# A weight piece's remainder on GpSimd: one subtraction of 1024 columns, or four of 256

## The chip, the cores and the metric

The kernel runs on one core of a Trainium2 chip. The metric is the device time of one execution in microseconds; a change is judged by the median of several runs. A core has TensorE (matrix products), VectorE, ScalarE and GpSimd (elementwise work), and queues that start DMA transfers between the chip's main memory and the on-chip SBUF; most of these transfers are started on SP's queue. Each engine works through its own instructions in order and waits on semaphores for the others.

## The reference: what is computed

Two layers of a diffusion backbone over 512 latent and 256 context tokens of 1024 features, in float32. In each layer:

```
h  = modulate(rms_norm(x, g_norm_attn[l]), sh1, sc1)
lat = prep_stream(h @ w_in[l], ...)          # q, k, v of three attentions, three gates
y  = (sigmoid(ga) * (y_mla @ w_up_mla) + sigmoid(gb) * (y_swa @ w_up_swa)
      + sigmoid(gc) * (y_diff @ w_up_diff)) @ w_o
x  = x + g1 * y
x  = x + g2 * (square(relu(modulate(rms_norm(x, g_norm_mlp[l]), sh2, sc2) @ w_mlp_in)) @ w_mlp_out)
```

The context tokens pass through the same weights in the first layer and are only read as keys and values in the second. The attentions are a latent attention of 8 heads, a windowed one of 8 heads with a sink, and a differential one of 4 heads.

## The kernel before, in words

Products run on float32r operands. Every float32 operand is split into a rounded half (hi) and a remainder (lo), and three products are summed in PSUM: hi with hi, hi with lo, lo with hi (lines 218 to 220 for weights that stand still, 481 to 483 for weights that move).

Weights come in pieces of 128 partitions by up to 1024 columns, made by `piece` (line 189): SP's queue loads the piece into one of two raw slots (tag wr), ScalarE copies it rounded into wh (line 197), and GpSimd subtracts that from the raw piece to give wl (line 199). There are four slots for wh and wl, so that up to four pieces are made ahead of TensorE. A piece is called for 266 times: 254 of 1024 columns, 8 of 832, 4 of 768. In the MLP a piece holds eight blocks of 128 columns, each the fixed operand of three products for each stretch of up to 512 tokens; in the projections by chunks (lines 481 to 483) it holds four blocks of 256 columns.

The work of a layer goes through four phases: projections with norms of heads and rotations (phase 1); attention, with the gate products filled in between its steps (phase 2); the three up-projections merged under the gates, and the output projection (phase 3); the MLP (phase 4), beside which the modulation of later parts is summed on VectorE (line 252).

What VectorE does between the products matters below. In attention: the maximum of the scores (line 908), the scaling of the probabilities by their sum (line 920), the difference of two maps (line 1066), the remainder of transposed probabilities (line 869). In the merge: the gate times the product (line 1232), the sum over branches (line 1238, on VectorE in the third branch and on GpSimd in the second), the remainder (line 1213). In the norms: three Newton steps of an rsqrt on a few columns (lines 443 to 454), each step needing the one before it, and the normed features (lines 431 and 434). In the MLP: the remainder of the squared activation (line 1307, behind GpSimd's square of line 1306) and the residual (line 1261).

The program is written in program order; a planner sets the order of instructions on each engine when the kernel is built, from priorities and a model of their times, and places the semaphore waits. That order is fixed when the kernel runs. Only the first norm's products are put on TensorE in an order written by hand. How the gate products are spread over the attention is set by the constants F1, WD and WC.

Of the kernel before, what the change touches and what calls it, by code (L numbers as in the profile page):

```python
"""Two layers of the hybrid diffusion backbone (MLA + windowed GQA + differential attention).

The residual stream is kept transposed (features on partitions, tokens on the free axis, latent
tokens first, context tokens after them).  Products run in float32r: every float32 operand is split
exactly into a rounded part and a remainder, and the three products that matter at float32
accuracy (hi*hi, lo*hi, hi*lo) are accumulated in PSUM.
"""
# [7 lines left out]
F32 = mybir.dt.float32  # L15
# [4 lines left out]
ALU = mybir.AluOpType  # L20
# [14 lines left out]
# columns of w_in  # L35
C_QLAT, C_KVLAT, C_KPE, C_SQ, C_SK, C_SV, C_DQ, C_DK, C_DV, C_G = (
    0, 256, 384, 416, 928, 1056, 1184, 1696, 2208, 2720)
# rope order of a head: [first halves of row and column | second halves of row and column]
# [3 lines left out]
# broadcast vectors of a layer  # L42
V_MQ, V_MK, V_SQ, V_SK, V_DQ, V_DK, V_SINK, V_L = 0, 96, 192, 256, 320, 384, 448, 456
NV = 456 + 256
# per-partition vectors of a layer
P_GA, P_GM, P_BM, P_GQ, P_GKV, P_GS = 0, 8, 16, 64, 66, 67
NP_ = 68
# constants
# [30 lines left out]
def _layout(inp):  # L79
    """Host side: permutations and concatenations only."""  # L80
    g = {n: np.asarray(a) for n, a in inp.items()}
    f = lambda a: np.ascontiguousarray(a, dtype=np.float32)
    o = {}
# [3 lines left out]
    # units of four feature blocks: shift and scale of the first norm by pairs of feature tiles, then kinds 2, 4 and 3  # L87
# [6 lines left out]
    w = g["w_in"]  # L94
# [42 lines left out]
class Build:  # L137
    def __init__(self, tc, ins, out):
        self.tc = tc
        self.nc = tc.nc  # L140
        self.ins = ins
        self.out = out
        self.n = 0
        self.mq = []
        self.early = False
        self.gains = {}
        self.F1, self.WD, self.WC = 0.3, 1.5, 0.4   # how the gates are spread over the attention
        self.px = 0

# [11 lines left out]
    def R(self, name, dt=F32):  # L161
        """a [128, 768] tile of the phase's pool"""
        return self.ph.tile([128, 768], dt, tag="R", bufs=self.NR, name=self.nm(name))
# [7 lines left out]
    def psx(self, name):  # L171
        """one bank for a dense product, from both tags in turn"""
        self.px += 1
        if self.px % 3 == 2:
            return self.psS(name)[:, 0:512]
        return self.psm(name) if self.px % 3 == 0 else self.psd(name)
# [12 lines left out]
    def piece(self, src, n=1024, own=0):  # L189
        """hi, lo of a piece of weights; own: the number of slots it takes of the phase's pool in place of the common  # L190
        ones."""
        nc = self.nc
        raw = self.sp.tile([128, 1024], F32, tag="wr", bufs=self.WR, name=self.nm("wr"))
        nc.sync.dma_start(raw[:, :n], src)
        pool, bufs = (self.ph, own) if own else (self.sp, self.WH)
        hi = pool.tile([128, 1024], F32R, tag="wh", bufs=bufs, name=self.nm("wh"))
        nc.scalar.activation(out=hi[:, :n], in_=raw[:, :n], func=AF.Copy)  # L197
        lo = pool.tile([128, 1024], F32R, tag="wl", bufs=bufs, name=self.nm("wl"))
        nc.gpsimd.tensor_tensor(out=lo[:, :n], in0=raw[:, :n], in1=hi[:, :n].bitcast(F32), op=ALU.subtract)  # L199
        return hi, lo  # L200

    def mm3(self, out, ah, al, bh, bl, start, stop):
        """out += (ah + al).T @ (bh + bl) but for al.T @ bl."""
        mm = self.nc.tensor.matmul
        mm(out, lhsT=ah, rhs=bh, start=start, stop=False)
        mm(out, lhsT=ah, rhs=bl, start=False, stop=False)
        mm(out, lhsT=al, rhs=bh, start=False, stop=stop)
# [5 lines left out]
    def dense_steps(self, ps, w, x, c):  # L213
        """ps = sum of w.T @ x[:, c]; w: [(hi, lo)] stationary [128, 128] blocks, x: [(hi, lo)] moving."""
# [8 lines left out]
    def split_sb(self, src, n=768):  # L223
        """hi, lo of an SBUF tile."""
# [7 lines left out]
    def mod_start(self, kinds):  # L232
        """queue up mod = silu(c) @ w_mod + b_mod for the given sixths, features on partitions."""
# [27 lines left out]
    def mod_pe(self, w, ks, ps):  # L261
        """ps[32 g + stream, 128 features] += 2 silu(c) @ w for four feature blocks g; w [128, len(ks), 512]."""
# [7 lines left out]
    def mod_out(self, ps, pt):  # L270
        """[128 features, 4 blocks, 32]: twice the modulation without its bias."""
# [5 lines left out]
    def mod_first(self, q):  # L277
        """shift and scale of the first norm for feature tiles 2q and 2q + 1, in two steps."""
# [18 lines left out]
    def mod_units(self, n):  # L297
        """n pieces of the modulation of kinds 2, 4 and 3 of the first layer."""
# [18 lines left out]
    def first_norm(self, x, h):  # L317
        """the first norm, feature tiles as their modulation arrives, and the query latent of the first layer: PSUM
        tiles [128 tokens, 256]."""
# [45 lines left out]
    def norm_gain(self, l, which, s, k=None):  # L365
        """128 * g * (1 + scale) per feature (rows_rsq gives 1 / 128); of feature tiles k and k + 1 alone at every even k."""
# [19 lines left out]
    def add_square(self, acc, x, j, c, sq, eng):  # L386
        """acc += x_j ** 2 on columns c; sq: a scratch tile."""
# [7 lines left out]
    def rows_rsq(self, sq, nt, ones, s=None):  # L395
        """sq [128 features, nt * 128 tokens] of squares -> [128, nt * 128]: rsqrt(mean + eps) of the tokens on the
        diagonal of every block, with eps * s ** 2 if the rows are s times too large. ones: column constant 1 / number
        of features."""
# [11 lines left out]
    def rows_bcast(self, dg, nt, name):  # L410
        """PSUM [128, nt * 128]: the diagonals of dg / 128 on all partitions."""
# [7 lines left out]
    def norm_apply(self, acc, x, h, c, gain, shift, hold):  # L419
        """h = split(x * rsqrt(mean) * gain + shift) on columns c; hold: the last scratch tiles take the slots of the  # L420
        modulation's weights, whose stream then starts after the norm."""
# [16 lines left out]
    def rsq_small(self, ss, n, d, s=None):  # L438
        """rsqrt(ss / d + eps) on [128, n]; rsqrt(ss + eps * s ** 2) if s is given."""
# [17 lines left out]
    def sumsq(self, raw, m, d):  # L457
        """sum of squares of raw [128, m * d] over d."""
# [12 lines left out]
    def bproj(self, act, w, n, tiles, evac):  # L471
        """act: [(hi, lo)] per k with tokens on the free axis; w: [(hi, lo)] per k, [128, n]."""
# [20 lines left out]
    def rope_pairs(self, raw, npair, nt, tab, gain):  # L493
        """raw [128, npair, nt, 2, 64]: gain and rotation of the latent tiles, gain alone of the context tiles."""
# [18 lines left out]
    def phase1(self, l, h, nq, pre):  # L513
# [5 lines left out]
        # rope tables with the gains in  # L519
# [22 lines left out]
        # MLA tables: [C | S] for q and k, 32 wide  # L542
# [26 lines left out]
        # q latent  # L569
# [11 lines left out]
        # kv latent, shared rope key, SWA keys and values  # L581
# [14 lines left out]
        def lora(raw, kts, nt, gcol):  # L596
            """raw [128 tok, nt, kts * 128] -> normalised, transposed and split."""
# [22 lines left out]
        # SWA keys  # L620
# [5 lines left out]
        # shared rope key  # L626
# [15 lines left out]
        def chunk256(ci, tiles):  # L642
            """a chunk of 256 columns of w_in, as [128, 2 pairs, tiles, 128]."""
# [25 lines left out]
        # MLA keys and values  # L669
        kw = []  # L670

        def ukv(ci):
# [16 lines left out]
            # ss index (pair, t, h)  # L689
# [20 lines left out]
        # MLA queries  # L710
# [48 lines left out]
        # P: what the attention needs for its first head  # L759
# [13 lines left out]
    def transp(self, tok, w, nt, evac):  # L773
        """token tiles of tok [128, nt, w] transposed; evac(ps, cols) for every PSUM bank."""
# [27 lines left out]
    def q_pair(self, tok, nt):  # L802
        """stacks [hi; lo] of head 0 and [lo; hi] of head 1."""
# [10 lines left out]
    def k_pair(self, d):  # L814
        """[hi; hi] and [lo; lo] of both heads of d: every head is loaded twice."""
# [19 lines left out]
    def v_heads(self, tok):  # L835
        """[hi | lo] of the two heads of a pair [128, 6, 128]."""
# [15 lines left out]
    def p_transpose(self, p, kts, PT, q2):  # L852
        """blocks kts of p (at column order of kts) into PT hi/lo [128, 6, 256] at half q2."""
# [19 lines left out]
    def pv2(self, v, PT, kts, y, rows, c):  # L873
        """y[rows, c] = (v_hi + v_lo).T @ (p_hi + p_lo) with v = [hi | lo]."""
# [28 lines left out]
    def exp_rows(self, ps, c0, sums):  # L903
        """exp(s - max) and its sums."""
# [23 lines left out]
    def mla_job(self, sc, hd, nq, st):  # L928
        """closures of a head: prep, units [(front, back)], ends."""
# [37 lines left out]
    def swa_job(self, l, sc, hd, nq, st):  # L967
# [16 lines left out]
        def unit(b):  # L984
# [17 lines left out]
            def front():  # L1002
                # the products are -s: p holds mask - s with -sink in front of it, the minimum is minus the maximum of the scores
# [30 lines left out]
    def diff_job(self, l, sc, hd, nq):  # L1034
# [16 lines left out]
        def unit(i):  # L1051
# [5 lines left out]
            def front():  # L1057
                # -s1 (p1 / s1 - lam p2 / s2): the norm of the head takes s1 out again, gsub the sign
# [46 lines left out]
    def gate_steps(self, l, h, nq, gates):  # L1105
        """tanh(logit / 2) of all gate features, kept in DRAM; yields after every step of three products."""
# [21 lines left out]
    def phase2(self, l, h, sc, nq, job, st):  # L1128
# [13 lines left out]
        def fill(t):  # L1142
            """dense work of t us between the steps of the attention"""
# [62 lines left out]
    def merge(self, l, br, ys, yh, gates, m, nq, psum):  # L1206
        """m += (1 + tanh) * (y @ w_up) for a branch; the last one returns 0.5 * m split, the others the next y split."""
# [55 lines left out]
    def out_proj(self, l, mh, x, nq, done):  # L1263
        """x += g1 * (m @ w_o); the last feature tiles run half by half; done(acc, c) after each half."""
# [28 lines left out]
    def mlp(self, l, h, x, nq, pre, fin, done):  # L1293
        """x += g2 * relu(h @ w_mlp_in) ** 2 @ w_mlp_out; fin(j, c) when x[j][:, c] is final."""
# [66 lines left out]
    def build(self):  # L1361
        tc, nc, ins = self.tc, self.nc, self.ins
        import contextlib
        with contextlib.ExitStack() as es:
# [13 lines left out]
            # conditioning  # L1378
            nc.scalar.preload_act_table_set("exp_and_others")
            # 2 silu(c) with the rows of w_mod on partitions  # L1380
# [96 lines left out]
    def norm(self, l, which, x, acc, h, c, hold=False):  # L1477
        """h[:, c] = modulated norm of x[:, c]"""
# [4 lines left out]
    def layer_consts(self, l):  # L1483
        """per-layer vectors, the lambda of the differential maps and the gain of their norm."""
# [45 lines left out]
```

## Time and profile before

| what | value |
| --- | --- |
| median of 3 runs | 2549.3 us (2545.8 to 2554.59) |
| span of the profiled execution | 2547.0 us |
| time of that execution around its span | not given apart; the median of the runs stands 2.3 us above the span |
| mean granted TensorE clock | 0.988 |
| instructions | 40061, of these GpSimd 629 |
| VectorE, ScalarE, GpSimd busy | 1537.6, 1079.7, 915.1 us |
| line 199 (the subtraction) | 266 instructions, 652.6 us |

In the profile PE is TensorE, PEld its weight loads, DVE VectorE, ACT ScalarE, POOL GpSimd and SPq SP's queue. An instruction's time runs from its start on the engine to its end, so time in which an engine is held up inside an instruction counts as busy. A row's releaser (after the arrow in brackets) is what ended the idle time before it. The granted clock is 1.00 at 2.4 GHz and 0.50 at 1.2 GHz.

### The profile page before, as it was taken

To read this page: it belongs to the slowest core of one execution; us is meant where nothing else is said; L and a number is where in the kernel's file an instruction comes from. 1 tells how busy PE (TensorE), PEld (TensorE's weight loads), DVE (VectorE), ACT (ScalarE), POOL (GpSimd) and SP (SyncE) were. 2 spreads that over 40 slices of the span, in tenths; PEclk is the share of its full clock that TensorE was granted. 3 is DMA by queue.
4 is the path that set the end of the run, shared out by engine and by line. 5 is a ranking of instruction groups with operands and counts; after the bars stand their busy time and mean duration, and the time that the engine had idled before them with its cause. 6 is when DMAs were issued, how large, how long until landed. Compare 5 with 4: busy or idle time off the path is not lost. (4 is left out here: it accounts for less than half of the span.)

```text
span 2547.0 us, 40061 instructions
## 1 busy us (share of the span) xinstructions
PE 2432.5 (96%) x15466; PEld 2136.6 (84%) x15466; DVE 1537.6 (60%) x3081; ACT 1079.7 (42%) x2105; POOL 915.1 (36%) x629
## 2 busy tenths in 40 slices
PE   6999999999999998999999989999999999999999
PEld 5989888888888887888888989998878777888888
DVE  6547777878874479872222277777788874621112
ACT  4343566667652233212222244346666632422321
POOL 2434211111115326434333354441222235454543
PEclk9999999999999999999999999999999999999999
DMA  7265322222346225662111122443323344222222
GB/s 280 90 222 203 131 97 84 96 77 94 100 137 226 94 76 171 214 231 75 59 67 66 60 99 86 173 153 95 103 83 118 110 156 155 83 92 99 91 100 83
DMA packets 133182, 307.38 MB, mean 121 GB/s; under 512 B 43264, under 2 KB 49536, under 8 KB 132608
## 3 DMA queue, kind: packets, MB, share of 16 engines
q1 hardware_dynamic: 122624, 281.23, 32.6%
q10 hardware_dynamic: 10368, 23.60, 2.4%
q8 instruction: 122, 2.00, 0.3%
q14 instruction: 68, 0.56, 0.1%
HBM read 252.08 MB, written 52.70 MB: 120 GB/s over the span
## 5 line engine op out<-in xcount | busy, mean ns | idle before, releaser
L199 POOL TENSOR_TENSOR wl<-wr,wh 128x1024 fp32r<-128x1024 f32 (+2 forms) x266 | 652.6, 2457 | 1139.2 <-ACT wh L197 1066.8
L197 ACT ACTIVATE wh<-wr 128x1024 fp32r<-128x1024 f32 (+2 forms) x266 | 279.5, 1052 | 581.2 <-PE mo L219 317.6
L218 PE MATMUL mo<-uh,wh 128*128 128x512 f32 (+1 forms) x832 | 286.4, 344 | 18.6 <-DVE x L1261 13.6
L219 PE MATMUL mi<-hl,wh 128*128 128x512 f32 (+1 forms) x832 | 285.7, 344 | 3.3 <-DVE hl L434 3.3
L220 PE MATMUL mi<-hh,wl 128*128 128x512 f32 (+1 forms) x832 | 285.2, 343 | 0.0
L218 PE MATMUL mi<-hh,wh 128*128 128x512 f32 (+1 forms) x832 | 284.8, 344 | 0.3 <-DVE x L1261 0.3
L219 PE MATMUL mo<-ul,wh 128*128 128x512 f32 (+1 forms) x832 | 283.8, 341 | 0.0
L220 PE MATMUL mo<-uh,wl 128*128 128x512 f32 (+1 forms) x832 | 283.1, 341 | 0.0
L1307 DVE TENSOR_TENSOR ul<-u,uh 128x512 fp32r<-128x512 f32 (+1 forms) x104 | 80.7, 777 | 304.0 <-POOL u L1306 301.7
L1261 DVE SCALAR_TENSOR_TENSOR x<-mo,mod,x 128x512 f32<-128x512 f32 (+1 forms) x208 | 127.9, 625 | 200.6 <-PE mo L220 200.6
L481 PE MATMUL pb<-wh,hh 128*128 128x256 f32 (+1 forms) x832 | 244.2, 294 | 0.0
L482 PE MATMUL pb<-wl,hh 128*128 128x256 f32 (+1 forms) x832 | 243.2, 292 | 0.8 <-POOL wl L199 0.8
L483 PE MATMUL pb<-wh,hl 128*128 128x256 f32 (+1 forms) x832 | 243.3, 293 | 0.0
L218 PE MATMUL g<-hh,wh 128*128 128x512 f32 (+1 forms) x576 | 212.2, 368 | 0.0
L220 PE MATMUL g<-hh,wl 128*128 128x512 f32 (+1 forms) x576 | 211.8, 368 | 0.0
L219 PE MATMUL g<-hl,wh 128*128 128x512 f32 (+1 forms) x576 | 211.5, 367 | 0.0
L868 ACT ACTIVATE pth<-pT 128x512 fp32r<-128x512 f32 (+3 forms) x344 | 154.1, 462 | 101.7 <-PE pT L865 90.4
L218 PEld LDWEIGHTS mo<-uh,wh 128*128 128x128 f32 x832 | 157.3, 189 | 39.1 <-DVE x L1261 14.9
L869 DVE TENSOR_TENSOR ptl<-pT,pth 128x512 fp32r<-128x512 f32 (+3 forms) x344 | 171.9, 516 | 24.8 <-ACT pth L868 22.6
L219 PEld LDWEIGHTS mi<-hl,wh 128*128 128x128 f32 x832 | 157.3, 189 | 23.5 <-DVE hl L434 3.7
L218 PEld LDWEIGHTS mi<-hh,wh 128*128 128x128 f32 x832 | 156.8, 189 | 20.4 <-DVE x L1261 0.5
L220 PEld LDWEIGHTS mi<-hh,wl 128*128 128x128 f32 x832 | 157.3, 189 | 19.8
(243 smaller groups left out, 5932.5 us busy)
## 6 DMA issues: line engine op xcount, KB each, us to landing
wr<-in_wmi SPq DMA_DIRECT2D x64, 512.0 KB, 3.5
wr<-in_wmo SPq DMA_DIRECT2D x64, 512.0 KB, 3.5
wm<-in_wmod SPq DMA_DIRECT2D x56, 512.0 KB, 3.6
wr<-in_wg SPq DMA_DIRECT2D x48, 512.0 KB, 3.6
wr<-in_wb SPq DMA_DIRECT2D x36, 512.0 KB, 4.2
wm<-in_wm SPq DMA_DIRECT2D x28, 512.0 KB, 4.5
wr<-in_wup SPq DMA_DIRECT2D x24, 512.0 KB, 3.5
gd<-gt ACTq DMA_DIRECT2D x24, 384.0 KB, 2.4
```

What stands on the lines that cost most here:

```text
L197: nc.scalar.activation(out=hi[:, :n], in_=raw[:, :n], func=AF.Copy)
L199: nc.gpsimd.tensor_tensor(out=lo[:, :n], in0=raw[:, :n], in1=hi[:, :n].bitcast(F32), op=ALU.subtract)
L218: mm(ps, lhsT=wh, rhs=xh[:, c], start=i == 0, stop=False)
L219: mm(ps, lhsT=wh, rhs=xl[:, c], start=False, stop=False)
L220: mm(ps, lhsT=wl, rhs=xh[:, c], start=False, stop=i == n - 1)
L481: mm(ps[:, :n], lhsT=ah[:, cs], rhs=wh, start=k == 0, stop=False)
L482: mm(ps[:, :n], lhsT=ah[:, cs], rhs=wl, start=False, stop=False)
L483: mm(ps[:, :n], lhsT=al[:, cs], rhs=wh, start=False, stop=k == nk - 1)
L868: nc.scalar.activation(out=hv[:, k0:k0 + n, qs], in_=pv, func=AF.Copy)
L869: nc.vector.tensor_tensor(out=lv[:, k0:k0 + n, qs], in0=pv, in1=hv[:, k0:k0 + n, qs].bitcast(F32), op=ALU.subtract)
L1261: self.nc.vector.scalar_tensor_tensor(out=x[j][:, c], in0=ps, scalar=g, in1=x[j][:, c], op0=ALU.mult, op1=ALU.add)
L1307: nc.vector.tensor_tensor(out=b[:, c], in0=u, in1=a[:, c].bitcast(F32), op=ALU.subtract)
```

## The change

The subtraction of line 199 is put into a loop over blocks of 256 columns. A piece of 1024 columns takes four instructions on GpSimd, one of 832 takes four (the last of 64 columns), one of 768 takes three. The load and ScalarE's copy stay whole. Comments and docstrings are taken out as well, which changes nothing in the program.

```
         lo = pool.tile([128, 1024], F32R, tag="wl", bufs=bufs, name=self.nm("wl"))
-        nc.gpsimd.tensor_tensor(out=lo[:, :n], in0=raw[:, :n], in1=hi[:, :n].bitcast(F32), op=ALU.subtract)
+        for o in range(0, n, 256):
+            c = slice(o, min(o + 256, n))
+            nc.gpsimd.tensor_tensor(out=lo[:, c], in0=raw[:, c], in1=hi[:, c].bitcast(F32), op=ALU.subtract)
         return hi, lo
```

## Rows read from the trace of the kernel before

**Rows 1.** The page's busy times by engine: us, share of the span, instructions.
```profile
PE 2432.5 (96%) x15466; PEld 2136.6 (84%) x15466; DVE 1537.6 (60%) x3081; ACT 1079.7 (42%) x2105; POOL 915.1 (36%) x629
```

**Rows 2.** Windows by stage: length, busy us of each engine, clock, DMA share, GB/s.
```profile
0.00:260.00 260.00, 230.92 (x2158) 217.01 (x2159) 163.07 (x373) 105.92 (x204) 98.86 (x93) 0.99 0.55 198
345.00:745.00 400.00, 389.22 (x2599) 339.97 (x2597) 321.90 (x771) 264.52 (x612) 67.57 (x61) 1.00 0.29 95
1005.00:1115.00 110.00, 94.39 (x514) 81.58 (x514) 95.78 (x137) 22.19 (x32) 45.94 (x22) 0.94 0.63 212
1470.00:1640.00 170.00, 151.44 (x1081) 147.75 (x1080) 134.36 (x296) 74.33 (x157) 82.59 (x79) 0.95 0.34 119
1640.00:2075.00 435.00, 420.13 (x2666) 356.78 (x2665) 344.36 (x708) 266.16 (x550) 118.31 (x93) 0.99 0.35 113
2075.00:2180.00 105.00, 98.44 (x472) 80.70 (x473) 51.76 (x74) 27.79 (x38) 50.33 (x27) 0.95 0.43 148
2200.00:2547.00 347.00, 343.89 (x1630) 286.42 (x1628) 79.97 (x114) 100.58 (x133) 176.68 (x94) 1.00 0.27 94
```

**Rows 3.** TensorE's waits: us in total, times, longest.
```profile
PE pm L266 <- DVE acc L393: 15.2, 1, 15.2
...
PE pb L482 <- POOL wl L199: 0.8, 2, 0.6
```

**Rows 4.** Timeline around a stall at 744: start us, us, what [idle before].
```profile
741.77 2.42 POOL L199 TENSOR_TENSOR wl<-wr,wh 128x1024 fp32r<-128x1024 f32 x1 [14.76 <-PE s L893]
...
742.18 2.29 DVE L1066 SCALAR_TENSOR_TENSOR p<-p,sm,p 128x256 f32<-128x256 f32 x1
...
745.12 0.39 PE L205 MATMUL o<-pth,vh 128*128 128x256 f32 x1 [1.31 <-DVE ptl L869]
```

**Rows 5.** Four VectorE lines: count, ns at least/median/at most, first and last start.
```profile
L1066 DVE SCALAR_TENSOR_TENSOR p<-p,sm,p x40: 484/1016/2287, 616.5 to 2060.4; 128x768 f32<-128x768 f32 x32, 128x256 f32<-128x256 f32 x8
...
L1238 DVE TENSOR_TENSOR m<-m,tl x16: 691/960/3128, 821.9 to 2134.3; 128x768 f32<-128x768 f32 x8, 128x512 f32<-128x512 f32 x8
...
L1232 DVE SCALAR_TENSOR_TENSOR tl<-tl,up x48: 406/678/689, 788.2 to 2133.5; 128x512 f32<-128x512 f32 x32, 128x256 f32<-128x256 f32 x16
...
L453 DVE SCALAR_TENSOR_TENSOR a<-a,v x135: 145/168/2340, 20.4 to 2194.9; 128x24 f32<-128x24 f32 x36, 128x6 f32<-128x6 f32 x24, 128x16 f32<-128x16 f32 x24, 128x2 f32<-128x2 f32 x24
```

**Rows 6.** GpSimd's groups by form: busy us, mean ns | idle before.
```profile
L199 POOL TENSOR_TENSOR wl<-wr,wh 128x1024 fp32r<-128x1024 f32 x254 | 628.3, 2476 | 1114.9 <-ACT wh L197 1045.6 <-DVE q L811 22.5 <-PE pT L865 17.0
...
L393 POOL TENSOR_TENSOR acc<-acc,sq 128x256 f32<-128x256 f32 x19 | 14.3, 754 | 16.9 <-ACT sq L392 10.8 <-ACT acc L390 5.7
```

**Rows 7.** Timeline of GpSimd and VectorE, 1557.7 to 1561.5, GpSimd instructions back to back.
```profile
1557.70 0.71 POOL L503 TENSOR_TENSOR rt<-raw,tab 128x256 f32<-128x256 f32 x1
1557.79 0.65 DVE L453 SCALAR_TENSOR_TENSOR a<-a,v 128x4 f32<-128x4 f32 x1
1558.38 0.71 POOL L504 TENSOR_TENSOR rt<-raw,tab 128x256 f32<-128x256 f32 x1
1558.48 0.64 DVE L454 SCALAR_TENSOR_TENSOR y<-a,y 128x4 f32<-128x4 f32 x1
...
1559.74 1.71 POOL L504 TENSOR_TENSOR rt<-raw,tab 128x256 f32<-128x256 f32 x1
```

**Rows 8.** The page's groups of two of the three products.
```profile
L219 PE MATMUL mo<-ul,wh 128*128 128x512 f32 (+1 forms) x832 | 283.8, 341 | 0.0
L220 PE MATMUL mo<-uh,wl 128*128 128x512 f32 (+1 forms) x832 | 283.1, 341 | 0.0
```

**Rows 9.** Timeline of VectorE within the stall at 1015.
```profile
1014.02 3.24 DVE L252 CUSTOM_DVE_ANT_0 dump<-wm,silu 128x1024 bf16<-128x1024 f32 x1
```

**Rows 10.** Timeline of TensorE behind the first and last of thirteen stalls.
```profile
1717.27 0.38 PE L881 MATMUL o<-pth,vv 128*128 128x256 f32 x1 [0.57 <-DVE ptl L869]
...
2065.98 0.39 PE L205 MATMUL o<-pth,vh 128*128 128x256 f32 x1 [1.47 <-DVE ptl L869]
```

**Rows 11.** Window of the low clock behind the stall at 2134.
```profile
2134.35:2141.18 6.83, 3.69 (x9) 2.63 (x9) 3.91 (x3) 2.32 (x3) 2.82 (x2) 0.50 0.23 79
```

## The prediction

> **What bounds the kernel.** Read the busy shares first: TensorE works 2432.5 of the 2547.0 us span, VectorE 60%, GpSimd 36% [rows 1]. So the order of the matmuls sets the time, and all that a change off TensorE can give back is the 114.5 us in which TensorE stands still, plus what a lowered clock costs. Next the windows by stage [rows 2], where the length minus TensorE's busy time is what to look at: 29.1 us idle in the first 260 us, 10.8 in 345 to 745 (layer 0's attention), 15.6 in 1005 to 1115 (the head of its MLP), 18.6 in 1470 to 1640 (the crossing to layer 1), 14.9 in 1640 to 2075 (layer 1's attention), 6.6 up to its output projection, 3.1 in its MLP; the stretches between hold the other 15.9. Then TensorE's own waits [rows 3]: 15.2 us are the start, before any weight piece, and for the remainder piece that the change touches TensorE waits 0.8 us in all. The weight supply is not what ends last.
>
> What does end last is VectorE. The timeline of one stall [rows 4] shows the pattern: the subtraction runs from 741.77 to 744.19; a VectorE update of 256 columns starts at 742.18 and is over at 744.47, just behind it; the next VectorE instruction feeds TensorE, which has stood for 1.31 us. The same line takes 0.48 us at its fastest, and the sum of line 1238 goes from 0.69 to 3.13 us, while line 1232, which reads PSUM as one input, never passes 0.69 [rows 5]. So a VectorE instruction that reads SBUF twice is held until the GpSimd instruction in progress has ended; the scaling of line 920, with one SBUF input, behaves alike. Going through TensorE's stalls of over 0.4 us, I find an instruction held by line 199 in front of most of them.
>
> **The change, part by part.** *Removed:* 266 subtractions, 254 of them of 1024 columns at 2.476 us. *Added:* four blocks for each piece of 1024 or 832 columns, three for 768. The nearest row of 256 columns on GpSimd is the sum of line 393, 0.754 us [rows 6]. So 4 x 0.754 = 3.02 for 2.48, 0.54 more a piece; over 254 pieces 137 us, and some 5 for the other 12: GpSimd goes from 915 to about 1057 us, 41% of the span. From the other side, back-to-back instructions of 256 columns start every 0.68 us [rows 7]: 2.72 a piece, 61 us more in all. I take the larger. It lies beside matmuls: a piece of an MLP feeds 24 products and more, of 0.21 us each in layer 1 (343.89 us over 1630 matmuls [rows 2]), 5.1 us, against 3.0 of GpSimd for the piece and about 1.1 for the piece's share of line 1306; and the first block is ready 0.75 us after the start where its columns came after 2.48. If that cover were gone, the cost would be up to 142 us; with 0.8 us of waits now I price it at nothing.
>
> *More waits on TensorE:* up to three more points a piece, some 800, at which line 220 and its like wait for GpSimd; all later matmuls queue behind such a wait. Today line 220 does so in one product of 13, line 219 never, and both last 341 ns with no idle time ahead [rows 8]: a wait that cost 13 ns would show as 1. So 0, at most 10 us; I take 0. *Queues:* the raw slot is let go 0.54 us later, and the next piece load on SP with it, with other loads behind it in that queue; the pieces in store cover that, 0 (the 142 us above if not).
>
> *What the stalls get back.* Held by a subtraction of 2.4 us, an instruction waits 1.2 us on average; held by a block of 0.75, 0.4, if VectorE comes in between two blocks. Rows 7 answer that: with GpSimd instructions of 0.71 us back to back, VectorE gets one instruction through for each (0.65 and 0.64 us, where such updates take 0.15 alone [rows 5]), and GpSimd waits in turn for a long VectorE one (1.71). So a single held instruction gains; a run of small dependent ones, as the steps of an rsqrt, does not: it is held once a block, 4 x 0.5 = 2.0 us, where it was held once for up to 2.2. Going through the stalls by that rule, estimates from the timeline:
> - 0 to 260: small chains and loads, -2 of 29.1.
> - 345 to 745: four stalls each behind one held scaling, two behind other single ones, -6.5 of 10.8; two more stand behind the unchanged subtraction of line 1046.
> - 1005 to 1115: the largest stalls (11.5 us) are a queue of modulation sums of 1.2 us, held to 3.2 [rows 9]; a dense stream alternates with blocks, so 0 there, and -2.5 of three later ones.
> - 1470 to 1640: -2.5 of 18.6, the rest being rsqrt runs, table work and results that wait for ScalarE.
> - 1640 to 2075: thirteen stalls behind a held instruction, the first of 0.57 us, the last of 1.47 [rows 10], -9.5 of 14.9.
> - 2075 to 2180: the sums of line 1238, held while the next product waits for the split of their result, -4 of 6.6.
> - Between these (two norms, a merge): -5 of 15.9.
>
> That is -32. *The clock:* behind the stall at 2134 the granted clock is 0.50, 1.2 GHz of 2.4, for 6.8 us in which nine matmuls pass [rows 11]; 1005 to 1115 stands at 0.94, 1470 to 1640 and 2075 to 2180 at 0.95 [rows 2]. Some of these stretches should go with their stalls, -5. *What comes back:* a stall removed brings the next VectorE result closer, and GpSimd holds on for 142 us more; I keep 70%: (32 + 5) x 0.7 = 26, and give one back for the rsqrt runs. The span goes from 2547.0 to 2522; the runs' median stood 2.3 us above that span: 2524.
>
> **A rule against it.** The Trainium skill, "GPSIMD Engine Reference", section Instruction dispatch, says that consecutive GpSimd instructions are no barrier: each of its cores takes up the next as soon as its own share is done. By that rule four blocks could hold the shared port like one instruction of 3 us; that is the first rival. Rows 7 speak against it here, since VectorE comes through once in each instruction of 0.71 us.
>
> **The rivals.**
> - *Held for the whole piece.* Blocks follow so closely that VectorE doesn't get in, and each hold grows from 2.48 to 3.02 us, by 22%. The stalls that follow VectorE, some 75 us (114.5 less the 15 at the start and some 25 behind loads, ScalarE and the end), grow with it: +17, 2566. It decides from the point at which no slot is left between two blocks. The one-for-one alternation of rows 7 is against it; that no four blocks of one piece are in this trace is for it. 0.11.
> - *One stall for another.* In dense stretches VectorE is hit by every block: four holds of 0.4 us are 1.6 a piece, more than one of 1.2. If streams and rsqrt runs set most stalls, what the single ones gain is spent there: 2549. For it speak 1005 to 1115 and 1470 to 1640 (34.2 us idle); against it, that some 25 stalls elsewhere have one held instruction each. 0.18.
> - *Nearly all goes.* A hold of 0.4 us falls within the lead that the filling products give, where 1.2 did not, and the clock stays up: two thirds of the 75 us, and some 5 of clock: 2495. The lengths in layer 1's attention (0.57 to 1.47 us) speak for it, the rsqrt runs against. 0.15.
> - The forecast, 2510 to 2541: 0.56.
>
> More GpSimd instructions may also put others in another order, on every engine; no row prices that, and it is in the width.
>
> **How the numbers follow.** 0.3% is 7.6 us, about what can be told from no change. Faster: the forecast and the large gain, 0.71; no difference: 0.18; slower: 0.11. The time is 2524. The range reaches down into the large gain and up over no change: 2498 to 2552.
>
> **What would show it.** Right: four times as many instructions of line 199, of about 0.75 us, and GpSimd near 1050; the longest instructions of lines 920, 1066, 1238 and 434 below 1.7 us; TensorE's idle time in 1640 to 2180 from 21.5 to below 11; lines 452 to 454 no better in sum; the clock at 1.00 in more of the stages. Wrong: VectorE instructions held for 2 us across several blocks; TensorE waiting for wl; as much idle time in new places, or matmuls in another order.

## The result, and the profile after

The changed kernel takes 2518.4 us (median of four runs, 2517.3 to 2521.0) against 2549.3 us. The ratio is 0.988 with a 95% interval of 0.986 to 0.989. The forecast was 2524. The profiled execution has a span of 2517.3 us against 2547.0. TensorE's matmuls stand in the same order in both traces. The planner moved some other instructions: on VectorE between 960 and 1160 us (layer 0's MLP) and within the norm at 1520, on SP two loads from 1140 us to 1018 and 1045, and a pair each at three places on ScalarE (742, 1525 and 2214 us of the kernel before). In the kernel after, line numbers from 200 on are higher by two (L1238 is L1240); in the kernels of the experiments they are as before.

The busy times by engine, with VectorE and GpSimd as [rows 1] have them:

```profile
PE 2425.4 (96%) x15466; PEld 2132.4 (85%) x15466; DVE 1498.0 (60%) x3081; ACT 1078.8 (43%) x2105; POOL 1102.9 (44%) x1423
```

GpSimd has 188 us more (1102.9 less 915.1) and VectorE 40 us less, for the same work: its instructions are held for shorter times. TensorE stands still for 91.9 us of the span, where it was 114.5 us, and is busy for 7.1 us less, at a higher mean granted clock (0.992 instead of 0.988). That is the 29.7 us.

The windows by stage follow. The stages are those of [rows 2], shifted so that each holds the same matmuls to within a few; columns are the length, busy us of each engine, clock, DMA share, GB/s.

```profile
0.00:262.00 262.00, 233.16 (x2159) 218.41 (x2160) 160.80 (x377) 106.03 (x204) 116.56 (x169) 0.99 0.55 196
346.00:742.00 396.00, 390.20 (x2603) 340.66 (x2601) 316.76 (x770) 264.46 (x611) 77.73 (x124) 1.00 0.29 96
1000.00:1108.00 108.00, 93.76 (x519) 80.78 (x518) 92.27 (x144) 22.29 (x32) 72.37 (x59) 0.95 0.67 226
1463.00:1625.00 162.00, 148.03 (x1079) 144.02 (x1080) 122.73 (x287) 74.25 (x157) 96.79 (x139) 0.97 0.33 114
1625.00:2056.00 431.00, 418.35 (x2667) 357.42 (x2666) 339.36 (x718) 265.22 (x550) 142.41 (x199) 0.99 0.36 118
2056.00:2152.00 96.00, 94.11 (x476) 78.58 (x476) 44.85 (x72) 28.14 (x39) 61.07 (x69) 1.00 0.47 162
2170.00:2517.00 347.00, 344.19 (x1632) 286.60 (x1631) 90.10 (x115) 100.86 (x133) 202.36 (x274) 1.00 0.27 94
```

The lengths go 260 to 262, 400 to 396, 110 to 108, 170 to 162, 435 to 431, 105 to 96, and 347 in both. So the crossing to layer 1 and the output projection before its MLP gave most, and the first stage lost. The low clock behind the stall at 2134 [rows 11] is gone: that stage runs at 1.00 instead of 0.95.

The VectorE lines of [rows 5] (count, ns at least/median/at most), and with them the norm's product L436:

```profile
L1068 DVE SCALAR_TENSOR_TENSOR p<-p,sm,p x40: 484/1012/2615, 614.5 to 2041.6; 128x768 f32<-128x768 f32 x32, 128x256 f32<-128x256 f32 x8
...
L1240 DVE TENSOR_TENSOR m<-m,tl x16: 691/960/1268, 818.7 to 2108.7; 128x768 f32<-128x768 f32 x8, 128x512 f32<-128x512 f32 x8
...
L436 DVE SCALAR_TENSOR_TENSOR hl<-nt,mod,hh x64: 464/481/970, 905.2 to 2173.3; 128x256 fp32r<-128x256 f32 x64
...
L455 DVE SCALAR_TENSOR_TENSOR a<-a,v x135: 147/174/726, 20.2 to 2165.3; 128x24 f32<-128x24 f32 x36, 128x6 f32<-128x6 f32 x24, 128x16 f32<-128x16 f32 x24, 128x2 f32<-128x2 f32 x24
```

Read the last of the three numbers. The sum of L1238 fell from 3.13 to 1.27 us at most, the rsqrt step from 2.34 to 0.73. L1068 still goes to 2.62: it stands there behind the unchanged subtraction of L1048, which lasts 1.85 us.

The stall of [rows 4], the same matmuls (start us, us, what, idle before):

```profile
739.28 3.01 POOL L201 TENSOR_TENSOR wl<-wr,wh 128x256 fp32r<-128x256 f32 x4 [14.33 <-PE s L895]
...
740.29 0.71 DVE L1068 SCALAR_TENSOR_TENSOR p<-p,sm,p 128x256 f32<-128x256 f32 x1
...
740.92 1.01 DVE L871 TENSOR_TENSOR ptl<-pT,pth 128x512 fp32r<-128x512 f32 x2
...
741.66 0.39 PE L207 MATMUL o<-pth,vh 128*128 128x256 f32 x1 [0.32 <-DVE ptl L871]
```

The four blocks take 3.01 us, and inside them VectorE gets its update done in 0.71 us where it took 2.29; TensorE waits 0.32 us instead of 1.31.

GpSimd's group of the changed line (busy us, mean ns | idle before), and a line of the products beside it that answers to [rows 8]:

```profile
L201 POOL TENSOR_TENSOR wl<-wr,wh 128x256 fp32r<-128x256 f32 x1060 | 847.2, 828 | 1014.5 <-ACT wh L197 959.4
...
L222 PE MATMUL mo<-uh,wl 128*128 128x512 f32 (+1 forms) x832 | 282.4, 340 | 0.0
```

The product pays nothing for its three more points of waiting: 340 ns as before (341). TensorE's waits (us in total, times, longest) show what is new:

```profile
PE pm L268 <- DVE acc L395: 14.9, 1, 14.9
PE mo L220 <- DVE x L1263: 12.6, 5, 10.0
...
PE tp L782 <- DMA ld<-km: 8.0, 2, 5.7
```

The 5.7 us is a stall that the kernel before did not have, at 1680: layer 1's first head waits for its keys. Timeline of GpSimd, VectorE and SP ahead of it, and of TensorE at its end:

```profile
1673.78 3.97 POOL L201 TENSOR_TENSOR wl<-wr,wh 128x256 fp32r<-128x256 f32 x5
1674.29 0.71 DVE L445 TENSOR_SCALAR v<-ss 128x16 f32<-128x16 f32 x1
1675.04 0.65 DVE L449 TENSOR_SCALAR y<-v 128x16 int32<-128x16 int32 x1
...
1677.12 0.66 DVE L455 SCALAR_TENSOR_TENSOR a<-a,v 128x16 f32<-128x16 f32 x1
1677.82 0.17 DVE L456 SCALAR_TENSOR_TENSOR y<-a,y 128x16 f32<-128x16 f32 x1
...
1679.28 1.22 DVE L470 TENSOR_TENSOR raw<-raw,y 128x1024 f32<-128x1024 f32 x1
1680.53 0.80 SPq L667 DMA_DIRECT2D qs<-raw  x2
...
1682.42 0.81 SPq L792 DMA_DIRECT2D ld<-km  x1
...
1686.46 0.84 PE L782 MATMUL tp<-identr,ld 128*96 128x128 f32 x6 [5.75 <-DMA ld<-km]
```

Two pieces, eight blocks, run there without a pause until 1677.8, and the steps of an rsqrt are held once a block: five in a row of 0.65 to 0.71 us, and 0.17 us each as soon as GpSimd stops. The product of L470 is late by that, a store of SP waits for it (the longest such wait of SP here is 5.1 us), and the loads of the head stand behind that store in SP's queue.

### The profile page after: what moved, and what is told of

Same layout as the page of the kernel before. It is cut to its first block, busy times and chain, and to the rows that moved or that the text cites. A ratio compares the mean times of both kernels' runs of the same rounds, so it can differ in the third digit from the quotient of the medians.

```text
span 2517.3 us, 40953 instructions
## 1 busy us (share of the span) xinstructions
PE 2425.4 (96%) x15466; PEld 2132.4 (85%) x15466; DVE 1498.0 (60%) x3081; ACT 1078.8 (43%) x2105; POOL 1102.9 (44%) x1423
## 5 line engine op out<-in xcount | busy, mean ns | idle before, releaser
L201 POOL TENSOR_TENSOR wl<-wr,wh 128x256 fp32r<-128x256 f32 x1060 | 847.2, 828 | 1014.5 <-ACT wh L197 959.4
L220 PE MATMUL mo<-uh,wh 128*128 128x512 f32 (+1 forms) x832 | 285.7, 343 | 15.6 <-DVE x L1263 12.6
L1309 DVE TENSOR_TENSOR ul<-u,uh 128x512 fp32r<-128x512 f32 (+1 forms) x104 | 96.1, 926 | 296.4 <-POOL u L1308 291.4
```

Of the source, the lines that this page charges most:

```text
L201: nc.gpsimd.tensor_tensor(out=lo[:, c], in0=raw[:, c], in1=hi[:, c].bitcast(F32), op=ALU.subtract)
L220: mm(ps, lhsT=wh, rhs=xh[:, c], start=i == 0, stop=False)
L1309: nc.vector.tensor_tensor(out=b[:, c], in0=u, in1=a[:, c].bitcast(F32), op=ALU.subtract)
```

## The experiments

*Theory T1, as forecast:* a VectorE instruction is held until the GpSimd instruction in progress ends, so the length of that instruction is what counts. *Rivals:* the number of instructions or the planner's new order did it (R1); the first block being ready sooner did it (R2). A second question came from the stall at 1680 and became the main one: is GpSimd's longer time free, as I had priced it (T2), or does it cost something (R3)?

**Instructions of uneven length.** Four instructions a piece again, three of 64 columns and one of 832, so that the number is as in the change and the longest hold nearly as before.

```
-  tensor_tensor(out=lo[:, :n], in0=raw[:, :n], in1=hi[:, :n], op=subtract)
+  for c in [slice(0,64), slice(64,128), slice(128,192), slice(192,n)]: tensor_tensor(out=lo[:, c], ...)
```

> Blocks of 64, 64, 64 and the remaining 832 columns: as many GpSimd instructions and semaphore points for a piece of 1024 as with four of 256, but one of them still holds VectorE for about 2 us. Every instruction of TensorE, VectorE, ScalarE and SP stands in the order of the kernel before. Theory of the hold (the time follows how long the longest GpSimd instruction keeps VectorE out): hardly any gain, 2540 to 2552. Rival, the number of instructions and the finer waits: near 2518 as with the four even blocks. If the 0.2 us of each further instruction cost something by themselves, over 2552.

Measured: 2542.6 us, ratio 0.996 (0.994 to 0.998). The sums and the norm's product in its trace:

```profile
L1238 DVE TENSOR_TENSOR m<-m,tl x16: 691/958/2682, 820.7 to 2131.2; 128x768 f32<-128x768 f32 x8, 128x512 f32<-128x512 f32 x8
...
L434 DVE SCALAR_TENSOR_TENSOR hl<-nt,mod,hh x64: 468/480/2248, 908.2 to 2200.2; 128x256 fp32r<-128x256 f32 x64
```

Single instructions of 2.2 and 2.7 us are back, where the same work takes 0.5 and 0.7 alone (2.6 and 3.1 were the longest in the kernel before), and most of the gain is gone. The number of instructions falls as a cause: as many of them, another length, 24 us apart. The planner's order is not settled by this run, for its kernel has the order of the kernel before on TensorE, VectorE, ScalarE and SP. The run with two blocks, below, bears on it.

**The blocks backwards.** As the change, the last 256 columns first; the columns that the first products want come last.

```
-  for c in [slice(o, min(o + 256, n)) for o in range(0, n, 256)]: ...
+  for c in [slice(o, min(o + 256, n)) for o in range(0, n, 256)][::-1]: ...
```

> The four blocks of 256 columns in reversed order, so that the columns that TensorE takes first are ready last. Theory of the hold: 2515 to 2523, as in the changed kernel (2518). Rival, the first block is ready early (0.75 us in place of 2.4) and that feeds TensorE: the gain goes back, 2535 to 2550, and TensorE waits for wl.

Measured: 2518.9 us, ratio 0.988 (0.985 to 0.991), the same as forwards. R2 falls.

**Two blocks of 512 and eight of 128.** The same line with another step.

```
-  ... range(0, n, 256) ...
+  ... range(0, n, 512) ...     (two)
+  ... range(0, n, 128) ...     (eight)
```

> Two blocks of 512 columns, each about 1.3 us. Theory of the hold: between the two, in proportion to the length of the hold 2549 - 31 x (2.40 - 1.29) / (2.40 - 0.74) = 2528, so 2522 to 2534; held VectorE instructions at most 1.3 us over their own time. Rival, any split does it: 2518. Rival, only a hold below some slack counts: 2540 and more.

Measured: 2526.9 us, ratio 0.991 (0.989 to 0.994), the longest of L1238 1.82 us, GpSimd 985 us: between one block and four, as the length of the hold has it. Its order is that of the change on TensorE and SP, and on VectorE but for a few instructions of the norm at 1520; yet it takes 8 us more. And in layer 0's attention and from 1640 us to layer 1's MLP, where 18 of the 30 us were gained, the change moved no more than one pair, on ScalarE. So the order is not what did it there; for the crossing and the head of layer 0's MLP, where instructions did move, the two are not told apart by stage. With that R1 falls for most of the gain.

> Eight blocks of 128 columns, each about 0.45 us (GpSimd some 1.0 us more per piece than with one). Theory of the hold alone: 2549 - 31 x (2.40 - 0.45) / (2.40 - 0.74) = 2512, so 2508 to 2517. Rival, the longer time of a piece on GpSimd and the later release of raw slots to SP's loads eats the rest: 2518 to 2530, with waits of TensorE for wl or for loads behind it.

Measured: 2527.6 us, ratio 0.991 (0.989 to 0.994), GpSimd 1298 us. The holds are shorter in sum than with four (VectorE has 44 us less; the longest rsqrt step, 0.78 us, and the longest of L434, 0.97, are as there), yet it is slower. One instruction was kept out for long:

```profile
2089.27 4.73 DVE L1238 TENSOR_TENSOR m<-m,tl 128x512 f32<-128x512 f32 x1
2090.07 3.38 POOL L199 TENSOR_TENSOR wl<-wr,wh 128x128 fp32r<-128x128 f32 x8
```

The first row's 4.73 us spans all eight blocks of a piece: VectorE did not get in between any of them. It is the only one of its 16 at that length, and it can't explain 9 us alone. (The last section has more such cases.) So shorter holds stop paying between 256 and 128 columns, and something that grows with the number of blocks takes it back: GpSimd's time is the candidate (R3).

**Four blocks again, and the first heads' loads on ScalarE's queue.** A run of the change beside three variants.

> The change as it is (four blocks of 256), beside the next three on the same chip: 2518, as before within 4 us. In its trace the loads of layer 1's first head stand behind a piece load in SP's queue and TensorE waits some 5.7 us for them at 1680.

Measured: 2520.8 us, ratio 0.988 (0.986 to 0.989).

```
-  self.nc.sync.dma_start(t[:, :n], d)
+  (self.nc.scalar if self.early else self.nc.sync).dma_start(t[:, :n], d)
```

> Four blocks, and the loads for the first head of each layer's attention started on ScalarE's queue in place of SP's, so that they don't stand behind piece loads that wait for GpSimd to release a raw slot. Theory (the later release of raw slots makes these loads late): the waits of TensorE for these loads (5.7 in layer 1, some 2 to 3 in layer 0) go, 2509 to 2514, that is 4 to 9 below the four blocks. Rival, the loads come as late for another reason (their source is written late), or ScalarE's queue takes the place: no difference to the four blocks.

Measured: 2518.6 us, ratio 0.987 (0.985 to 0.989): the intervals overlap. Its TensorE waits:

```profile
PE pb L481 <- ACT raw L650: 3.6, 1, 3.6
PE tp L780 <- DMA ld<-km: 2.9, 1, 2.9
```

The stall at layer 1's loads, 6.4 us in the run beside it, is gone (the 2.9 us is the one at layer 0's first head, 2.2 there), and a wait for a ScalarE result of 3.6 us came in its place, 50 us earlier. ScalarE's rows ahead of that wait:

```profile
1625.79 0.36 ACTq L790 DMA_DIRECT2D ld<-vm  x1
1626.61 0.39 ACT L650 ACTIVATE raw<-pb 128x256 f32<-128x256 f32 x1 [9.01 <-DVE raw L468]
```

ScalarE stands for 9.0 us and goes on right behind the load, where in the run beside it line 650 runs from 1618.9 us on. So the stall goes through SP's queue, but taking it away is not worth 6 us: the loads hold up ScalarE instead. (The planner also put 119 matmuls in another order in this kernel, some of them at 1620 to 1714.)

**The other subtraction in blocks too.** The change, and line 1046 in three blocks.

```
-  nc.gpsimd.tensor_tensor(out=vl, in0=vt, in1=vh, op=subtract)
+  for c in (slice(0,256), slice(256,512), slice(512,768)): nc.gpsimd.tensor_tensor(out=vl[:, c], ...)
```

> Four blocks, and the other long subtraction on GpSimd (the remainder of the values in the differential attention, 8 times 768 columns, 1.85 us) in three blocks of 256. The order on TensorE, VectorE, ScalarE and SP is that of the four blocks. Theory of the hold: the two stalls behind it in layer 0 (0.4 and 1.1 us) shorten, some 1 us in all, 2514 to 2519. Rival: nothing.

Measured: 2514.6 us, ratio 0.986 (0.984 to 0.988). It is the fastest median of all, as the theory wants, but its interval overlaps that of four blocks alone; the gain is not shown.

**One block twice.** The change, and the last block of each piece done once more: 0.75 us more of GpSimd a piece, with no longer hold.

```
-  for c in [... range(0, n, 256)]: ...
+  for c in [... range(0, n, 256)] + [slice(n - 256, n)]: ...
```

> Four blocks of 256 and the last one once more: the length of a hold as with four, but a piece takes 0.75 us more of GpSimd, some 200 us in all, as much as eight blocks of 128 took (1298 us of GpSimd against 1103). If eight blocks lost their 9 us by the longer time of a piece on GpSimd: 2523 to 2532 here too, and waits for wl as there (8.6 us). If they lost it by VectorE being kept out across several short blocks: 2515 to 2522 here.

Measured: 2569.2 us, ratio 1.007 (1.005 to 1.009). Both expectations were far off: 48 us above four blocks, and 42 above eight, with nearly eight's GpSimd time. The page:

```profile
PE 2448.5 (95%) x15466; PEld 2149.9 (84%) x15466; DVE 1522.9 (59%) x3081; ACT 1079.1 (42%) x2105; POOL 1323.3 (52%) x1689
```

TensorE idles 119.4 us (91.7 in the four blocks beside it) and is busy for 23 us more (2425.2 there), at a lower mean granted clock (0.982 instead of 0.992). Either GpSimd's time costs that much, and eight blocks earned it back by their shorter holds, or the block written twice at the end is special. Four more kernels tell this apart.

*The first block twice, ahead of the others.*

```
+  for c in [slice(0, min(256, n))] + [... range(0, n, 256)]: ...
```

> Four blocks of 256 columns, and the FIRST block is done once more ahead of them (five had the last one once more: 2569, the same GpSimd time as the eight blocks of 128, which took 2528). The repeated work writes what it wrote before. Theory T (it is GpSimd's time itself: some 210 us more of 256-column instructions make whatever stands behind them on GpSimd late, and eight blocks only paid it back with shorter holds): 2560 to 2575, as five. Rival L (in five the piece's end was late because the last columns were written twice, one behind the other): 2520 to 2535.

Measured: 2568.2 us, ratio 1.008 (1.006 to 1.009), as with the last one. Which block of the piece is done twice makes no difference.

*Eight blocks, the last two twice.*

```
+  for c in [... range(0, n, 128)] + [... range(max(n - 256, 0), n, 128)]: ...
```

> Eight blocks of 128 columns, and the last two of them once more: to the eight blocks what five is to four, a repeated 256 columns, in instructions of 128. GpSimd some 1540 us. T: eight (2528) plus what the repeat cost on four (some 48 us): 2565 to 2585. Rival H (what the repeat costs is one more hold of VectorE of .75 us a piece, and short instructions hold it less): 2532 to 2548.

Measured: 2579.5 us, ratio 1.012 (1.011 to 1.014), 52 us above eight: the same 256 columns cost as much in instructions of half the length. So the price is not that of one more hold of 0.75 us. Four VectorE instructions in its trace are held over six blocks and more (the last section); TensorE has no stall of over 0.3 us behind three of them and 1.5 us in all beside the fourth, so they are not the price either.

*The kernel before, the last 256 columns twice.*

```
-  tensor_tensor(out=lo[:, :n], ...)
+  for c in [slice(0, n), slice(max(n - 256, 0), n)]: tensor_tensor(out=lo[:, c], ...)
```

> The kernel before (the whole piece in one instruction), and the last 256 columns once more behind it. GpSimd some 1110 us, as with four blocks, but with holds of 2.4 us still. T: 2549 plus some 45: 2585 to 2605. Rival H: the long holds are there as before, one of .75 is added: 2552 to 2575.

Measured: 2596.3 us, ratio 1.020 (1.017 to 1.022), 48 us above the kernel before. The price was there already, before anything was cut.

*Four blocks, the last 64 columns twice.*

```
+  for c in [... range(0, n, 256)] + [slice(max(n - 64, 0), n)]: ...
```

> Four blocks of 256, and the last 64 columns once more: some .31 us a piece, 82 us of GpSimd in all, against 210 in five. T, in proportion to GpSimd's time: 2520 plus 48 x 82/210 = 2539 (2533 to 2545). If the price is only paid beyond some spare time of GpSimd at single places: 2518 to 2528. If it is paid by the number of instructions or by the rewriting as such: 2555 to 2572.

Measured: 2536.9 us, ratio 0.996 (0.995 to 0.998): it goes with GpSimd's time, not with the number of instructions.

The page's VectorE and GpSimd times of the last three:

```profile
PE 2448.4 (95%) x15466; PEld 2146.2 (83%) x15466; DVE 1495.4 (58%) x3081; ACT 1078.9 (42%) x2105; POOL 1550.8 (60%) x3007
```

```profile
PE 2444.1 (94%) x15466; PEld 2143.0 (83%) x15466; DVE 1593.0 (62%) x3081; ACT 1080.0 (42%) x2105; POOL 1143.6 (44%) x895
```

```profile
PE 2434.7 (96%) x15466; PEld 2138.7 (84%) x15466; DVE 1497.2 (59%) x3081; ACT 1080.1 (43%) x2105; POOL 1210.7 (48%) x1689
```

Against the kernel that each stands on, by spans and GpSimd's busy time: the last block twice +51.0 us for +228 (2567.9 less 2516.9; 1323.3 less 1095.1), the first block twice +49.0 for +228, eight blocks +50.9 for +253, the kernel before +42.4 for +229, the 64 columns +17.4 for +116. That is 0.15 to 0.22 us for each us. T2 falls, R3 holds.

One more thing differs in these five kernels: the planner's order. Up to 28 matmuls at the head of layer 1's MLP moved by one or two places (2160 to 2174 us), VectorE's and SP's order changed in layer 0's MLP, VectorE's also in a norm or two, and SP's in a few places behind 1620 us. The price can't be only that. Ahead of 950 us TensorE, VectorE and SP run in one order in both of each pair, and by there the kernel with one block twice is 16.7 us behind four blocks, the one with the first block twice 17.4, eight blocks with two more 16.0 behind eight, the kernel before with its block 11.7 behind the kernel before, and the 64 columns 8.2 behind four. For the rest the order may have a part in the price.

*Where it is paid.* The windows of the kernel with one block twice, from the start to layer 0's attention, at the head of its MLP, at the crossing, in layer 1's attention and up to its output projection:

```profile
0.00:354.00 354.00, 317.76 (x2713) 293.04 (x2714) 223.70 (x501) 152.64 (x309) 168.16 (x228) 0.97 0.50 175
1012.00:1129.00 117.00, 96.69 (x515) 82.98 (x515) 95.77 (x148) 22.45 (x32) 83.64 (x74) 0.91 0.66 216
1485.00:1659.00 174.00, 152.34 (x1077) 148.00 (x1078) 125.71 (x287) 74.16 (x157) 111.24 (x156) 0.94 0.31 105
1659.00:2099.00 440.00, 422.96 (x2669) 360.69 (x2669) 347.09 (x718) 265.46 (x550) 173.43 (x237) 0.98 0.36 116
2099.00:2201.00 102.00, 97.72 (x470) 80.12 (x470) 45.40 (x70) 27.50 (x38) 73.44 (x84) 0.97 0.45 152
```

and of the four blocks beside it, the same matmuls:

```profile
0.00:342.00 342.00, 312.48 (x2715) 288.80 (x2716) 219.10 (x501) 152.08 (x309) 138.06 (x196) 0.99 0.52 181
996.00:1104.00 108.00, 92.81 (x513) 80.05 (x512) 89.26 (x141) 21.50 (x31) 69.59 (x58) 0.95 0.67 223
1459.00:1623.00 164.00, 149.75 (x1080) 146.17 (x1081) 121.27 (x287) 74.27 (x157) 95.98 (x139) 0.96 0.33 113
1623.00:2054.00 431.00, 418.10 (x2665) 357.04 (x2664) 339.69 (x718) 265.49 (x550) 140.35 (x199) 0.99 0.37 118
2054.00:2151.00 97.00, 94.44 (x471) 78.51 (x472) 46.08 (x71) 27.52 (x38) 60.50 (x69) 1.00 0.47 160
```

The lengths differ by 12, 9, 10, 9 and 5 us, 45 of the 51, at a lower clock in each; the rest of the two MLPs costs next to nothing (0.0 and 0.9 us). Only a small part of it is TensorE waiting for wl itself:

```profile
PE pb L482 <- POOL wl L199: 8.3, 7, 4.0
```

That wait has 8.3 us against 2.5 in the four blocks. The largest wait that grew is on SP: its piece loads wait for the subtraction that lets a raw slot go. First the kernel with one block twice, then the four blocks, then the eight (SP's waits: us in total, times, longest):

```profile
SPq L194 <- POOL wl L199: 892.9, 227, 12.7
```

```profile
SPq L194 <- POOL wl L199: 682.5, 222, 7.2
```

```profile
SPq L194 <- POOL wl L199: 872.6, 227, 12.1
```

That is 210 us more (the waits that end with ScalarE's rounding of the piece fell by 103, from 639.9 to 537.3, so 108 in sum), and the longest wait is 12.7 us instead of 7.2. But these waits don't measure the price: eight blocks have them at nearly the size of the kernel with one block twice (545.1 us on ScalarE's rounding beside the 872.6) and are 42 us faster. So it is not shown that the price goes through SP's queue. What reaches TensorE is spread over waits for VectorE and ScalarE results and for loads, and the clock behind them. How much comes of GpSimd's results being late, and how much of VectorE being kept out for a larger share of the time (it has 25 us more with one block twice, 55 in the kernel before with its block), no run here separates.

## Why the prediction was right, and where it was not

The total was right, 2518 for 2524, and so was the mechanism: the uneven lengths show that the hold by the instruction in progress is what the change takes away. That the sum came out within 6 us is in part luck: a cost was set to nothing, and the gain was set too small by an amount that, as far as can be estimated, is of about the same size.

- *Queues and cover, "0 (the 142 us above if not)".* This step failed. Time added on GpSimd is not free: at 0.15 to 0.22 us a us, its 188 us cost an estimated 28 to 41 us. The rates are those of repeated blocks; part of the 188 us is GpSimd waiting in turn for VectorE, and no run shows that this part costs as much. The argument looked at TensorE's wait for wl (0.8 us in [rows 3], 1.8 after), and with a block twice that wait grew by 5.8 of the 51 us only. The step named the queue as well and set it to nothing: the new load stall of 5.7 us came through it, behind a run of steps that eight blocks held. How the rest of the price reaches TensorE stays open.
- *What the stalls get back, 26 us.* Too small. The change gave 30 us after that price, so by the same estimate the shorter holds gave some 58 to 71. A comparison at equal GpSimd time shows the size: the whole piece with its block twice has 1143.6 us of GpSimd and a span of 2589.4; four blocks, between the kernels with 1095.1 (2516.9) and 1210.7 us (2534.3), would have 2524 there. The same columns in blocks are worth some 65 us, with what the planner's order has in it. That is about what the rival "nearly all goes" had, 50 for the stalls and 5 for the clock; if the estimate holds, its time did not come because GpSimd's took it back.
- *By stage,* as the first matmul behind each end of a stage moved: 0 to 260 forecast -2, +1.8 came (GpSimd has 18 us more there, and a block done twice cost most in the windows from the start); 345 to 745 -6.5, -4.6 came; 1005 to 1115 -2.5, -2.8 came; 1470 to 1640 -2.5, -7.7 came; 1640 to 2075 -9.5, -5.6 came; 2075 to 2180 -4 and the clock, -7.8 came. In 1640 to 2075 the stalls of over 0.4 us went from 14 with 15.6 us to 6 with 10.5; without the new one of 5.7 it is 4.8, so the term itself was right and the load stall took half of it.
- *The runs of an rsqrt "do not gain".* Wrong: the stall that such a run ends at 924 fell from 3.40 to 2.35 us, others by 0.2 to 1.6, and the busy time of lines 452 to 454 from 106.4 to 98.0 us. The stalls of this kind in the crossing at 1470 are part of why it gave three times its forecast. The rule of one for one does show, in the run at 1674, where two pieces come one behind the other; 4 x 0.5 a piece took that case for the usual one.
- *More waits on TensorE, 0.* Right: 340 ns where it was 341.
- *The blocks' time, 4 x 0.754.* Low: 828 ns each, for GpSimd waits in turn while VectorE goes between two of them (at 1671 to 1675 us a block takes 1.18 to 1.20 us so, the next four 0.73 to 0.74). GpSimd has 1103 us and not 1057.
- *Signs.* The longest of L1238 and L434 are below 1.7 us as said (1.27 and 0.97), though in the later run of the same program one of L1238 took 2.69; those of lines 920 and 1066 are not (1.78 and 2.62), all behind line 1046. TensorE's idle time in 1640 to 2180 fell from 21.5 to 14.5 us, not below 11, by the load stall. The clock is at 1.00 in one stage more.
- *The first rival.* VectorE is not held over the whole piece as a rule, but single instructions are, in the change too (the last section). The rule of the Trainium skill that I had put against the change ("GPSIMD Engine Reference", section Instruction dispatch) describes how GpSimd starts its instructions; here four blocks mostly let VectorE in between them, as the 0.71 us update inside 3.01 us of blocks shows, so the hold did not grow to 3 us for each piece. Whether it has to do with the few long holds, no run shows.

## What to carry to other kernels

An instruction on GpSimd that VectorE has to wait out is worth cutting, but each cut adds to the engine's own time, and there is a best size: here 256 columns (0.75 us) beat 512 and 128. Before cutting, price the engine's own time: add one useless block and time it, and see in the trace what else moved with it; one run of the kernel before would have shown 0.2 us for each us of an engine that was busy 36% of the span. A direct wait of 0.8 us for an engine's result does not say that the engine has time to spare.

## What was not expected of the hardware

VectorE mostly gets an instruction in after each GpSimd one, but not always. The 4.73 us in the kernel of eight blocks, for a sum that takes 0.69, is not the only case. In the run of four blocks, the change itself, a sum of the same line waits out three blocks:

```profile
2084.55 2.69 DVE L1238 TENSOR_TENSOR m<-m,tl 128x512 f32<-128x512 f32 x1
```

```profile
2083.88 2.82 POOL L199 TENSOR_TENSOR wl<-wr,wh 128x256 fp32r<-128x256 f32 x4
```

The trace of the first run of that program has none, so it is not fixed by the order; the runs with the blocks backwards, with the loads on ScalarE's queue and with the other subtraction in blocks have one each, of 2.68 to 2.76 us, at the same place. In eight blocks with the last two twice there are four such instructions of 3.6 to 9.9 us, over 6 to 19 blocks. One of them:

```profile
2134.01 7.11 DVE L1238 TENSOR_TENSOR m<-m,tl 128x512 f32<-128x512 f32 x1
```

```profile
2136.32 4.25 POOL L199 TENSOR_TENSOR wl<-wr,wh 128x128 fp32r<-128x128 f32 x10
```

What makes these different was not found.
